# A two-layer attention trunk on one core: gate sums, squares and the last addition change engines, and the list of issue is new

## The chip, the cores and the metric

The kernel runs on one core of one Trainium2 chip. The metric is the device time of one execution in microseconds (us), lower is better. Three executions of the kernel before gave 297.03, 297.08 and 297.94 us, median 297.08. A fourth execution was profiled: it took 296.7 us, of which the profile covers a span of 294.8 us from its first to its last instruction.

## What is computed

The reference is a decoder trunk of two layers over one sequence of 256 tokens, 1024 wide, in fp32:

```
c_act = silu(c)
for layer in range(2):
    shift, scale, gate = split(c_act @ w_ada[layer] + b_ada[layer], 3)
    h = rms_norm(x, norm_g[layer]) * (1 + scale) + shift
    y = even_mixer(h, ...) if layer == 0 else odd_mixer(h, ...)
    x = x + gate * y
return rms_norm(x, final_g)
```

The even mixer projects h with one matrix of 1024 x 2968, runs 8 heads of window attention with sinks and 8 heads of sparse attention (compressed, selected and window branches), multiplies each branch by a SiLU gate path and projects the result with a 1024 x 1024 matrix. The odd mixer does the same with 16 heads of block attention. At this length the selected blocks cover everything that the causal mask leaves, so the kernel computes causal attention there. What matters for the change: gate is a row of 1024 numbers for each layer, made of c_act and a 1024 x 1024 block of w_ada; each rms_norm needs the sum of squares of every row of x; and the output is rms_norm of the x that the second layer leaves.

## The kernel before

The 256 tokens are two tiles of 128 partitions. Weights are 70 MB and are read once. A product in fp32 precision is made of three passes: every operand is split into a rounded part (hi, written by ScalarE as a CAST) and a rest (lo, written by VectorE as a subtraction), and `mm3` (line 576) issues hi x hi, hi x lo and lo x hi. So each 128 x 1024 block of weights costs one ScalarE CAST (`whi<-raw`), one VectorE TENSOR_TENSOR (`wlo<-raw,whi`) and TensorE's three passes over it. Five buffers `raw` take the weights from DMA, four `whi` and four `wlo` hold the split ones; of TensorE's eight accumulators three are called `ps_pj`, two `ps_s`, and one each `ps_pt`, `ps_o` and `ps_m`.

All engine calls go through a recorder (`Plan`, its `record` at line 226), which numbers them and notes what each depends on. `issue` (line 256) then emits them in the order of a long list of numbers, `ORDER` (line 38 on). This list sets how the work of the stages is interleaved on every engine and in which order SP issues the DMAs; each engine then works its own instructions off strictly in that order. Since all instructions leave through one line of the recorder, the profile shows L253 for nearly everything, and the names of the tiles tell what an instruction is.

The stages in order of time, with the names that the prediction uses:

- Start: the norm of x, the shift and scale of layer 0 and the projection of most of the even columns, as the weights arrive.
- The softmax stage of layer 0: six groups of four heads' scores. For each group TensorE makes scores, VectorE takes the row minimum (CUSTOM_DVE, listed as ISA in the order), ScalarE the exponential, VectorE and ScalarE scale (`sm<-sm,rc`), TensorE transposes and multiplies with the values. Gate paths (`ps_pj<-hhi,whi` of 256 columns), and, from `jobs` (line 1164) by `fill`, the ada work are put between.
- The ada work makes rows of c_act @ w_ada in one of two ways, chosen by a letter in `G0_ON`, `SS_ON` and `G1_ON` (lines 26 to 28). Letter "v" (`ada_sums`, line 446): for 512 columns, eight blocks of `raw` are each multiplied by a column of c and summed up in the tile `acc`, the first on ScalarE, the other seven on VectorE (SCALAR_TENSOR_TENSOR `acc<-raw,cz,acc`); for a gate, `ada_gate` (line 504) splits acc, and two matmuls with a matrix of ones (`ones_r`) sum over the partitions. Letter "p" (`ada_rows`, line 429): for 256 columns, eight matmuls on TensorE (`ps_m<-raw,cz`) make partial rows, ScalarE copies them (`asb`), and one matmul with `selbc` adds them up and spreads them.
- The projection out of layer 0 (`out_proj`, line 1188), in two halves of 512 columns. Its second half goes to `ps_s`, one accumulator for each tile of tokens. `add_scaled` (line 378) multiplies by gate, adds to x (the tile `xs`) and sums squares into `parts`.
- The boundary: for each tile of tokens, `inv_root` (line 402) raises the mean square to the power -1/2 on GpSimd, VectorE scales the first 512 columns of x (`t<-xs,parts`) and ScalarE the others, TensorE transposes them (`ta` holds the identity), and the result is scaled, shifted and split into `hhi` and `hlo`, the operands of layer 1.
- Layer 1 in the same manner, and its projection out (from line 1257), whose last piece is tile 1's columns 768 to 1023. Behind it stands the end of the kernel: add x, square with a sum, square root, reciprocal, multiply by `final_g` (`fg`, in `bigA`) and by the reciprocal, and two DMAs, of columns 0 to 383 from ScalarE's queue and of the rest from SP's.

Of the kernel before, what the change touches and what calls it, by code (L numbers as in the profile page):

```python
# [13 lines left out]
P = 128  # L14
# [12 lines left out]
G0_ON = "vp"  # L27
# [237 lines left out]
def tile_trunk(  # L265
# [136 lines left out]
    def inv_root(part):  # L402
        G.tensor_tensor(part[:, 3:4], part[:, 2:3], ex0[:, 0:1], ALU.pow)
        return part[:, 3:4]
# [952 lines left out]
```

## Time and profile before

| what | value |
|---|---|
| median of three executions | 297.08 us (297.03 to 297.94) |
| the profiled execution: its time, its span | 296.7 us, 294.8 us |
| TensorE matmul / weight load busy | 284.1 us (96%) / 242.6 us (82%) |
| VectorE / ScalarE / GpSimd busy | 246.0 (83%) / 194.6 (66%) / 9.1 us (3%) |
| chain that ended last: TensorE, DMA, VectorE | 88%, 4%, 3% |
| mean granted clock of TensorE | 0.99 |

An instruction's row in the profile gives its start and its length in us. The engines overlap the end of one instruction with the beginning of the next, so two rows of one engine in a row start closer together than the first is long; what an added instruction costs is the distance of the starts. PE is TensorE's matmul, PEld its weight load, DVE is VectorE, ACT ScalarE, POOL GpSimd; SPq and ACTq are DMAs issued by SP and by ScalarE. An fp32 matmul that isn't split appears as two rows.

### The profile page before, as it was taken

The page shows a single profiled execution, that of the slowest core. Times are in us where ns is not written, and L with a number is a line of the kernel's source. Part 1 is how long each engine was busy: PE and PEld are TensorE (multiplying, and loading weights), DVE is VectorE, ACT ScalarE, POOL GpSimd, SP SyncE. Part 2 cuts the span into 40 slices and gives each one's busy share as a digit, 9 for nine tenths or more (in the row PEclk, how much of TensorE's full clock was granted, in tenths as well). Part 3 has the DMA queues.
Part 4 walks back from the last instruction along what each step waited for, and adds up shares of the span by engine and source line. Part 5 has one row for each costly group of instructions (what it writes and reads, how often), then busy time and mean ns, then how long its engine had stood idle before and what let it go on. Part 6 is the DMA issues. An engine that isn't in the chain of part 4 may idle for free.

```text
span 294.8 us, 6255 instructions
## 1 busy us (share of the span) xinstructions
PE 284.1 (96%) x2326; PEld 242.6 (82%) x2326; DVE 246.0 (83%) x580; ACT 194.6 (66%) x461; POOL 9.1 (3%) x34
## 2 busy tenths in 40 slices
PE   6899999999999999999999999999999999999991
PEld 5677887999698877777757899999789989887891
DVE  0388798899999999989999569798846998899963
ACT  3477356765899999994458753664488358783832
POOL 4200000001000000000020000000000000000000
PEclk9799999999999999999999999999999999999998
DMA  7999999997799679579989628958466761721003
GB/s 238 374 387 380 374 396 365 353 326 244 211 359 336 230 238 329 194 241 295 286 265 311 201 74 273 344 185 267 143 217 213 218 238 49 259 99 73 0 0 142
DMA packets 62397, 71.69 MB, mean 243 GB/s; under 512 B 3416, under 2 KB 53024, under 8 KB 62368
## 3 DMA queue, kind: packets, MB, share of 16 engines
q1 hardware_dynamic: 61792, 70.78, 72.1%
q10 hardware_dynamic: 448, 0.48, 0.5%
q8 instruction: 18, 0.29, 0.4%
q14 instruction: 11, 0.09, 0.1%
q0 software_dynamic: 128, 0.05, 0.1%
HBM read 70.25 MB, written 1.05 MB: 242 GB/s over the span
## 4 chain that ended last, share of the span: by engine, by line
PE 88%; DMA 4%; DVE 3%; SPq 2%; issue 1%; POOL 1%; ACT 0%; DVEq 0%; ACTq 0%
PE ps_pj L253 57%; PE ps_s L253 11%; PE ps_pt L253 8%; PE ps_o L253 7%; PE ps_m L253 5%; DMA raw<-in_w_in_even_dram 2%; DMA qT<-in_w_ada_dram 2%; SPq L253 2%; DVE acc L253 1%; DVE t L253 1%; POOL parts L253 1%; DVE xs L253 0%; DVE wlo L253 0%; ACT whi L253 0%; ACT t L253 0%
## 5 line engine op out<-in xcount | busy, mean ns | idle before, releaser
L253 ACT CAST whi<-raw 128x1024 fp32r<-128x1024 f32 (+4 forms) x84 | 76.1, 917 | 45.8 <-PE ps_pj L253 20.3
L253 DVE TENSOR_TENSOR wlo<-raw,whi 128x1024 fp32r<-128x1024 f32 (+3 forms) x84 | 87.8, 1056 | 13.1 <-ACT whi L253 13.0
L253 PE MATMUL ps_pj<-hhi,whi 128*128 128x256 f32 x272 | 67.0, 284 | 0.0
L253 PE MATMUL ps_pj<-hlo,whi 128*128 128x256 f32 x272 | 66.7, 282 | 0.0
L253 PE MATMUL ps_pj<-hhi,wlo 128*128 128x256 f32 x272 | 66.6, 284 | 0.0
L253 PEld LDWEIGHTS ps_pj<-hhi,whi 128*128 128x128 f32 x272 | 47.9, 188 | 1.4 <-issue 0.7
L253 PEld LDWEIGHTS ps_pj<-hlo,whi 128*128 128x128 f32 x272 | 47.9, 188 | 0.8 <-issue 0.4
L253 PEld LDWEIGHTS ps_pj<-hhi,wlo 128*128 128x128 f32 x272 | 47.7, 188 | 0.3
L253 DVE SCALAR_TENSOR_TENSOR acc<-raw,cz,acc 128x512 f32<-128x512 f32 x42 | 31.3, 746 | 0.5 <-ACT acc L253 0.3
L253 ACT ACTIVATE sm<-sm,mn 128x256 f32<-128x256 f32 (+1 forms) x58 | 25.9, 449 | 4.9 <-DVE mn L253 4.9
L253 PE MATMUL ps_pj<-whi,hlo 128*128 128x512 f32 (+1 forms) x56 | 21.6, 396 | 0.0
L253 PE MATMUL ps_pj<-whi,hhi 128*128 128x512 f32 (+1 forms) x56 | 21.1, 398 | 0.5 <-ACT hhi L253 0.5
L253 PE MATMUL ps_pj<-wlo,hhi 128*128 128x512 f32 (+1 forms) x56 | 21.5, 396 | 0.0
L253 PE MATMUL ps_pj<-wlo,ghi 128*128 128x512 f32 (+1 forms) x56 | 20.4, 370 | 0.0
L253 PE MATMUL ps_pj<-whi,ghi 128*128 128x512 f32 (+1 forms) x56 | 20.0, 366 | 0.0
L253 PE MATMUL ps_pj<-whi,glo 128*128 128x512 f32 (+1 forms) x56 | 19.9, 364 | 0.0
L253 PE MATMUL ps_pt<-ta,sm 128*128 128x128 f32 x87 | 15.5, 277 | 0.0
L253 DVE TENSOR_TENSOR t<-ps_pj,tF 128x512 f32<-128x512 f32 x18 | 11.6, 683 | 4.5 <-PE ps_pj L253 4.5
L253 ACT COPY pT<-ps_pt 128x384 f32<-128x384 f32 x25 | 11.8, 474 | 3.0 <-PE ps_pt L253 2.7
L253 ACT ACTIVATE t<-xs 128x512 f32<-128x512 f32 (+2 forms) x9 | 6.1, 679 | 11.4 <-DVE xs L253 8.1
L253 PEld LDWEIGHTS ps_pt<-ta,sm 128*128 128x128 f32 x87 | 10.2, 140 | 3.2 <-issue 1.0
L253 PEld LDWEIGHTS ps_pj<-whi,hhi 128*128 128x128 f32 x56 | 10.4, 189 | 2.6 <-ACT hhi L253 0.7
(252 smaller groups left out, 590.9 us busy)
## 6 DMA issues: line engine op xcount, KB each, us to landing
raw<-in_w_in_odd_dram SPq DMA_DIRECT2D x32, 512.0 KB, 5.0
raw<-in_w_ada_dram SPq DMA_DIRECT2D x28, 512.0 KB, 5.7
raw<-in_w_in_even_dram SPq DMA_DIRECT2D x10, 512.0 KB, 7.1
t<-in_w_ada_dram SPq DMA_DIRECT2D x16, 256.0 KB, 5.8
raw<-in_w_out_even_dram SPq DMA_DIRECT2D x8, 512.0 KB, 6.0
raw<-in_w_out_odd_dram SPq DMA_DIRECT2D x8, 512.0 KB, 5.5
raw<-in_w_in_even_dram SPq DMA_DIRECT2D x8, 396.0 KB, 6.0
qT<-in_w_ada_dram SPq DMA_DIRECT2D x12, 256.0 KB, 6.0
```

The source lines that it names most:

```text
L253: self.ops.append(dict(key=eng.key, deps=deps, fn=lambda: getattr(real, name)(*args, **kw)))
```

## The change

The letters for layer 0's gate become "vv": the second 512 columns are now summed on VectorE and ScalarE like the first, not on TensorE. The sum of squares over the last half of x before the boundary is made by a ScalarE activation with an accumulator in place of a VectorE instruction with one, and `inv_root` adds the two halves first, with one small VectorE instruction. In the last piece of the kernel TensorE starts the accumulator with x itself, as identity times the split x (two matmuls), so that the square and the multiplication by `final_g` read the accumulator directly. And `ORDER` is another list. The few words that go with the change also name the second tile's scalings on ScalarE; the diff has no line that moves a scaling, and the lists of instructions hold the same scalings on the same engines before and after.

```
-G0_ON = "vp"
+G0_ON = "vv"
...
 ORDER = [int(i) for i in """
-0 4 74 8 10 3 5 11 2 12 9 6 13 1 14 15 7 77 16 17 34 75 59 60 22 35 61 36 18 19 44 62 38 30 81 45 78 20 21 46 63
...
         elif last:
-            V.tensor_tensor_reduce(
-                out=yt,
...
-                accum_out=part[:, 2:3],
-            )
+            A.activation(yt, xs[:, t, cs], AF.Square, scale=D**-0.5, accum_out=part[:, 2:3])
         else:
...
     def inv_root(part):
+        V.tensor_tensor(part[:, 2:3], part[:, 2:3], part[:, 0:1], ALU.add)
         G.tensor_tensor(part[:, 3:4], part[:, 2:3], ex0[:, 0:1], ALU.pow)
...
+    A.copy(hhi[:, 0, :P], ident)
+    A.copy(hhi[:, 1, :], xs[:, 1, 768:])
+    V.tensor_tensor(hlo[:, 1, :], xs[:, 1, 768:], hhi[:, 1, :].bitcast(F32), ALU.subtract)
...
+            held = done and t == 1
+            plan.fence("pe")
+            if held:
+                T.matmul(py[:, :256], hhi[:, 0, :P], hhi[:, 1, :], start=True, stop=False)
+                T.matmul(py[:, :256], hhi[:, 0, :P], hlo[:, 1, :], start=False, stop=False)
...
+            if held:
+                A.activation(t4()[:, :256], py[:, :256], AF.Square, scale=D**-0.5, accum_out=part[:, 1:2])
+                V.tensor_tensor(xs[:, t, cs], py[:, :256], fg[:, cs], ALU.mult)
+            else:
+                add_scaled(t, cs, py[:, : c1 - c0], part, done, n == 1)
+                V.tensor_tensor(xs[:, t, cs], xs[:, t, cs], fg[:, cs], ALU.mult)
```

Counted over the whole lists, TensorE loses 16 matmuls `ps_m<-raw,cz` and 2 `ps_m<-asb,selbc`, and gains 2 with `ones_r` and the 2 that bring in x. VectorE gains 7 `acc<-raw,cz,acc` and one `wlo<-acc,whi` of 512 columns, one multiplication of gate rows of 512 columns takes the place of two of 256, and 2 sums of squares go. ScalarE gains one `acc<-raw,cz`, one `whi<-acc` and 2 squares, and loses 2 copies `asb`; it also gains the 2 CASTs, and VectorE the subtraction, that split the identity and x near the end. SP issues as many DMAs as before. Between VectorE's first row minimum and its scaling of tile 0 at the boundary stand all of the 7 added sums: 35 rows `acc<-raw,cz,acc` there, 28 before.

The new list moves nearly everything by some places. Three places matter below. TensorE at the boundary, before: rows `ps_s_92` are tile 1's projection, `ps_pj_95<-ta,t_87` and `ps_o_97<-ta,t_87` tile 0's transposes, and `hhi` stands for the first rows of layer 1.

```order
L253 MATMUL ps_s_92<-wlo_114,ghi 128x512
L253 MATMUL ps_pj_95<-ta,t_87 128x128 x4
L253 MATMUL ps_s_92<-whi_110,glo 128x512
L253 MATMUL ps_o_97<-ta,t_87 128x128
L253 MATMUL ps_m_67<-ta,asb_107 128x128
L253 MATMUL ps_s_92<-whi_111,ghi 128x512
L253 MATMUL ps_m_67<-ta,asb_107 128x128
L253 MATMUL ps_s_92<-wlo_115,ghi 128x512
L253 MATMUL ps_s_92<-whi_111,glo 128x512
L253 MATMUL ps_s_92<-whi_111,ghi 128x512
L253 MATMUL ps_s_92<-wlo_115,ghi 128x512
L253 MATMUL ps_s_92<-whi_111,glo 128x512
```

The same place on TensorE after:

```order
L253 MATMUL ps_s_92<-wlo_116,ghi 128x512
L253 MATMUL ps_s_92<-whi_112,glo 128x512
L253 MATMUL ps_m_67<-raw_105,cz 32x256 x8
L253 MATMUL ps_pj_95<-ta,t_87 128x128 x4
L253 MATMUL ps_o_97<-ta,t_87 128x128
L253 MATMUL ps_m_67<-ta,asb_107 128x128 x2
L253 MATMUL ps_o_97<-ta,t_87 128x128 x3
L253 MATMUL ps_m_67<-raw_101,cz 32x256 x8
L253 MATMUL ps_pj_93<-whi_109,hhi 128x512
```

Before, 7 matmuls of tile 1's projection stand behind tile 0's first transposes; after, all of them stand ahead of these, and behind them only transposes and one group of ada rows come before layer 1.

VectorE at the same boundary, before: `ps_s_91,gate` is tile 0's last product with gate, the ISA rows are the sum of squares, and the TENSOR_SCALAR is tile 0's scaling, which waits for GpSimd's power.

```order
L253 TENSOR_TENSOR t_89<-ps_s_91,gate 128x512
L253 TENSOR_TENSOR shs<-ps_m_67,rT 128x2
L253 TENSOR_TENSOR xs<-t_89,xs 128x512
L253 TENSOR_TENSOR shs<-ps_m_67,rT 128x2
L253 ISA t_89,parts<-xs,parts 128x512
L253 ISA parts 128x1
L253 TENSOR_TENSOR wlo_116<-raw_104,whi_112 128x1024
L253 TENSOR_SCALAR t_87<-xs,parts 128x512
```

And after:

```order
L253 TENSOR_TENSOR xs<-t_89,xs 128x512
L253 TENSOR_TENSOR wlo_113<-raw_104,whi_109 128x1024
L253 TENSOR_TENSOR parts<-parts 128x1
L253 TENSOR_TENSOR shs<-ps_m_67,rT 128x2
L253 TENSOR_TENSOR t_90<-ps_s_92,gate 128x512
L253 TENSOR_SCALAR t_87<-xs,parts 128x512
```

The split of weights stood beside GpSimd's power and now stands ahead of the small addition that the power waits for; tile 1's product with gate (`t_90<-ps_s_92,gate`), which stood behind the scaling, now stands beside the power.

The end of the program on VectorE, after; `ps_pj_94` is the last piece's accumulator, which now holds x too.

```order
L253 TENSOR_TENSOR xs<-ps_pj_93,xs 128x256
L253 TENSOR_TENSOR xs<-ps_pj_94,bigA 128x256
L253 TENSOR_TENSOR xs<-xs,bigA 128x256
L253 RECIPROCAL parts<-parts 128x1
L253 TENSOR_SCALAR t_87<-xs,parts 128x640
```

Before, the second row was `xs<-ps_pj_94,xs`, the addition, and the reciprocal stood ahead of the multiplication by `final_g`; now both multiplications stand ahead of the reciprocal.

More of the change, by code (lines that the diff above doesn't have):

```diff
@@ L387, in add_scaled @@
         elif last:
-            V.tensor_tensor_reduce(
-                out=yt,
-                in0=xs[:, t, cs],
-                in1=xs[:, t, cs],
-                scale=1.0 / D,
-                scalar=part[:, 0:1],
-                op0=ALU.mult,
-                op1=ALU.add,
-                accum_out=part[:, 2:3],
-            )
+            A.activation(yt, xs[:, t, cs], AF.Square, scale=D**-0.5, accum_out=part[:, 2:3])
         else:
@@ L1270, in tile_trunk @@
             py = bank("pj")
-            plan.fence("pe")
-            for k in range(KT):
-                mm3(py[:, : c1 - c0], ghi[:, k, sl], glo[:, k, sl], ws[n][k][0][:, c0:c1], ws[n][k][1][:, c0:c1], k == 0, k == KT - 1)
             cs = slice(512 * n + c0, 512 * n + c1)
@@ L1276, in tile_trunk @@
             done = n == 1 and c1 == 512
-            add_scaled(t, cs, py[:, : c1 - c0], part, done, n == 1)
-            V.tensor_tensor(xs[:, t, cs], xs[:, t, cs], fg[:, cs], ALU.mult)
+            held = done and t == 1
[3 more added lines that the diff above has]
+                T.matmul(py[:, :256], hhi[:, 0, :P], hlo[:, 1, :], start=False, stop=False)
+            for k in range(KT):
+                mm3(py[:, : c1 - c0], ghi[:, k, sl], glo[:, k, sl], ws[n][k][0][:, c0:c1], ws[n][k][1][:, c0:c1], k == 0 and not held, k == KT - 1)
+            if held:
[4 more added lines that the diff above has]
+                V.tensor_tensor(xs[:, t, cs], xs[:, t, cs], fg[:, cs], ALU.mult)
             if done:
```

251 rows, old and new, of the table ORDER are left out of this document.

## The prediction

> **What bounds the kernel now.** I read the page first: its shares say which engines can be bounds at all.
>
> ```profile
> span 294.8 us, 6255 instructions
> PE 284.1 (96%) x2326; PEld 242.6 (82%) x2326; DVE 246.0 (83%) x580; ACT 194.6 (66%) x461; POOL 9.1 (3%) x34
> ```
>
> A share over the whole span mixes stages, so next come the windows, cut where the stages meet: the first scores at 72.5 us and tile 0's scaling at 150.8 us. The columns are the window, its length, then busy time and count of PE, PEld, DVE, ACT and POOL, the clock, the DMA share and GB/s.
>
> ```profile
> 20.00:72.50 52.50, 52.37 (x396) 46.03 (x394) 47.58 (x89) 31.39 (x69) 0.60 (x5) 1.00 1.02 351
> 72.50:120.00 47.50, 47.50 (x532) 38.11 (x533) 46.16 (x174) 45.28 (x148) 0.59 (x2) 1.00 0.88 289
> 120.00:150.80 30.80, 30.80 (x198) 22.74 (x194) 28.71 (x57) 21.76 (x49) 1.73 (x3) 1.00 0.77 237
> 160.00:210.00 50.00, 50.00 (x411) 46.30 (x410) 40.17 (x80) 27.30 (x49) 0.00 (x0) 1.00 0.65 208
> 210.00:288.60 78.60, 78.60 (x614) 70.18 (x612) 65.63 (x137) 50.13 (x111) 0.74 (x3) 1.00 0.42 141
> ```
>
> From 160 us on TensorE alone is full. In the softmax stage three engines are: VectorE is busy 46.16 + 28.71 = 74.87 of 78.3 us up to the boundary, ScalarE 45.28 of the first 47.5. A row of PE covers a pipelined matmul, so its busy time alone proves nothing; the timeline of TensorE in that stage (start, length, instruction, count) tells more.
>
> ```profile
> 99.73 0.28 PE L253 MATMUL ps_pj<-hhi,wlo 128*128 128x256 f32 x1
> ...
> 100.31 0.28 PE L253 MATMUL ps_pj<-hhi,wlo 128*128 128x256 f32 x1
> 100.52 1.07 PE L253 MATMUL ps_m<-raw,cz 128*32 128x256 f32 x16
> 101.53 0.66 PE L253 MATMUL ps_pt<-ta,t 128*128 128x128 f32 x4
> ...
> 102.96 0.59 PE L253 MATMUL ps_m<-asb,selbc 128*128 128x256 f32 x2
> 103.39 0.49 PE L253 MATMUL ps_pt<-ta,sm 128*128 128x128 f32 x3
> ```
>
> Starts follow without a hole: five steps of 0.58 / 5 = 0.116 us for 256 columns, 1.01 us for one group of ada rows, 0.43 us for one `selbc`. So TensorE is full there too. The kernel is bound by TensorE nearly throughout, with VectorE and ScalarE right behind it from 72 to 151 us; that is where the change puts work on the second and takes it from the first.
>
> **TensorE's sum.** A matmul of 512 columns costs 0.23 us by these two starts:
>
> ```profile
> 147.13 0.40 PE L253 MATMUL ps_s<-wlo,ghi 128*128 128x512 f32 x1
> 147.36 0.40 PE L253 MATMUL ps_s<-whi,glo 128*128 128x512 f32 x1
> ```
>
> Removed: two groups of ada rows, 2 x 1.01, and two `selbc`, 2 x 0.43: 2.88 us. Added: two matmuls with `ones_r`, 0.46, and the two that bring in x, 2 x 0.116 = 0.23. Net -2.2 us. The list moves other work across the stages, and counting its rows gives this split. Ahead of the first scores stand 7 fewer matmuls of 256 columns: -0.8 us, in a window where TensorE was busy 52.37 of 52.5. Between the first scores and tile 0's transposes stand those 7 and 7 matmuls of tile 1's projection out, so there -2.88 + 0.46 + 0.81 + 1.61 = 0.0. After the transposes: -1.61 + 0.23 = -1.4.
>
> **VectorE's sum.** All of its added work lies between the first scores and the boundary. Its timeline in the stage:
>
> ```profile
> 103.70 0.75 DVE L253 SCALAR_TENSOR_TENSOR acc<-raw,cz,acc 128x512 f32<-128x512 f32 x1
> 104.37 1.22 DVE L253 TENSOR_TENSOR wlo<-raw,whi 128x1024 fp32r<-128x1024 f32 x1
> 105.50 0.42 DVE L253 TENSOR_TENSOR gate<-ps_m,gate 128x256 f32<-128x256 f32 x1
> 105.84 0.68 DVE L253 SCALAR_TENSOR_TENSOR oT<-ps_o,oT 128x512 f32<-128x512 f32 x1
> 106.44 0.74 DVE L253 SCALAR_TENSOR_TENSOR acc<-raw,cz,acc 128x512 f32<-128x512 f32 x1
> ```
>
> By the starts a sum step costs 0.67, two inputs of 512 columns 0.60, the gate step of 256 columns 0.34. So: 7 x 0.67 = 4.7; the low part of the new acc 0.6; one gate step of 512 for two of 256, 0.6 - 0.7 = -0.1; tile 1's product with gate, moved ahead of the scaling, +0.6; the sum of squares that goes, -0.67 (148.43 to 149.10, below); the small addition, some 0.1. Together +5.2 us, where the windows leave 78.3 - 74.9 = 3.4 us idle. If all idle is used the stretch grows by 1.8; if none, by 5.2. It can also stay at TensorE's sum, 0.0: a row ends some 0.08 us after the next may start (0.75 shown, 0.67 spaced), so pauses shorter than that between the 231 rows don't show as idle. I take +1.2, between TensorE's 0.0 and the 1.8, since a new list is free to fill pauses of both kinds. ScalarE's first sum step, CAST and squares less two copies are under 2 us by its own rows of like size, the squares at the boundary; I take them as hidden.
>
> **The boundary.** Rows from the timelines of the engines; brackets give the idle time before an instruction and who ended it.
>
> ```profile
> 146.86 0.69 DVE L253 TENSOR_TENSOR t<-ps_s,gate 128x512 f32<-128x512 f32 x1 [0.18 <-PE ps_s L253]
> 148.43 0.75 DVE L253 CUSTOM_DVE_ANT_0 t<-xs,parts 128x512 f32<-128x512 f32 x1
> 149.10 1.22 DVE L253 TENSOR_TENSOR wlo<-raw,whi 128x1024 fp32r<-128x1024 f32 x1
> 149.26 1.48 POOL L253 TENSOR_TENSOR parts<-parts,expo 128x1 f32<-128x1 f32 x1 [2.22 <-DVE parts L253]
> 149.62 0.63 ACT L253 ACTIVATE t<-xs 128x512 f32<-128x512 f32 x1
> 150.77 0.49 DVE L253 TENSOR_SCALAR t<-xs,parts 128x512 f32<-128x512 f32 x1 [0.45 <-POOL parts L253]
> 151.32 0.66 PE L253 MATMUL ps_pj<-ta,t 128*128 128x128 f32 x4 [0.47 <-DVE t L253]
> 153.12 0.41 ACT L253 CAST hhi<-t 128x256 fp32r<-128x256 f32 x1 [1.63 <-DVE fs L253]
> 154.96 0.48 PE L253 MATMUL ps_pj<-whi,hhi 128*128 128x512 f32 x1
> 156.39 0.55 POOL L253 TENSOR_TENSOR parts<-parts,expo 128x1 f32<-128x1 f32 x1 [5.49 <-DVE fs L253]
> ```
>
> From the end of tile 0's projection (146.8) to the transposes are 4.5 us, and TensorE runs dry for 0.47 of them. The power took 1.48 us beside VectorE's `wlo` and 0.55 without such company. After the change: product 0.6, two small steps 0.2 (0.16 at most each, as the reciprocal below), addition 0.7; the square on ScalarE (0.63 and reading its sum) runs beside the `wlo` of 1.13 that now stands ahead; the small addition with its hand-overs 0.3, the power 0.55, beside a product that reads an accumulator; scaling 0.5: 4.0 us, and 4.5 if the power still waits for that product's end. The cover ahead of the transposes, 12 matmuls of tile 1 and an ada group, is 12 x 0.23 + 1.0 = 3.8. So the hole there stays at 0.2 to 0.7: no term. The Trainium skill, SBUF — State Buffer, "SBUF: two separate sides", has the lock behind these two rows: a VectorE instruction with two SBUF inputs and a GpSimd one that reads SBUF exclude each other for a whole instruction. By that rule the product, with one input in PSUM, doesn't hold up the power, and the hole would be the shorter; both rows agree with it.
>
> What the hole loses comes behind it. Before, the first row of layer 1 started 154.96 - 151.32 = 3.6 us after the transposes, and 7 matmuls, 1.61 us, filled that; now they stand ahead. What is left to TensorE there is two rows of four transposes, 0.66 each or somewhat less, and an ada group of 1.01, some 2 us, while the first CAST of `hhi` ended 2.2 us after the transposes began (153.53). Tile 1's transposes and the low parts come right after, with the same chance of a hole. I take 0.5 us idle in all, bounds 0 and 1.6.
>
> **The end.** The last matmul, and what follows it on each engine:
>
> ```profile
> 288.34 0.27 PE L253 MATMUL ps_pj<-whi,glo 128*128 128x256 f32 x1
> ...
> 288.65 0.42 DVE L253 TENSOR_TENSOR xs<-ps_pj,xs 128x256 f32<-128x256 f32 x1
> 289.17 0.42 ACT L253 ACTIVATE t<-xs 128x256 f32<-128x256 f32 x1 [1.29 <-DVE xs L253]
> ...
> 290.04 0.16 DVE L253 RECIPROCAL parts<-parts 128x1 f32<-128x1 f32 x1 [0.96 <-ACT parts L253]
> 290.12 0.41 DVE L253 TENSOR_TENSOR xs<-xs,bigA 128x256 f32<-128x256 f32 x1
> ...
> 290.56 0.55 DVE L253 TENSOR_SCALAR t<-xs,parts 128x640 f32<-128x640 f32 x1
> 290.88 0.35 ACTq L253 DMA_DIRECT2D out_dram<-t  x1
> 291.18 0.34 SPq L253 DMA_DIRECT2D out_dram<-t  x1
> ```
>
> The addition goes: the square can start at 288.65, 0.52 earlier, and ScalarE's DMA with it. On VectorE both multiplications (0.34 each) fit before the reciprocal at 289.52, so the last scaling comes 0.52 + 0.44 = 0.96 earlier and SP's DMA too. The span ends 3.62 us after SP's issue; ScalarE's DMA then is the later by 0.14. Gain 0.82 to 0.96, and 0.5 if the square is slower from an accumulator: -0.85. The two CASTs and the subtraction that split x lie in the last window, where ScalarE was busy 50.1 of 78.6 us and VectorE 65.6; nothing.
>
> **The sum.** -0.8 + 1.2 - 1.4 + 0.5 - 0.85 = -1.35 us. The profiled execution took 296.7, so 295.3 against it; the median 297.08 lies 0.4 above, and I give the median: 295.7. About 0.3%, 0.9 us, is what a measurement of this kernel can tell from no change.
>
> **The rivals.** TensorE's sum holds: the stretch up to the boundary keeps its 78.3 us, and layer 1 starts without a hole: -0.8 - 1.4 - 0.85 = -3.05, 294.0. For it speaks that VectorE was busy 97% of the time from 72.5 to 120 us while TensorE's starts followed without a hole, so a full VectorE needn't hold TensorE up; against it, that 5.2 us don't fit into the 3.4 shown.
>
> VectorE takes over, the one on the other side. If the new sums delay row minima and splits as they are, and its idle time of 3.4 us stays, the stretch grows by the whole 5.2: -0.8 + 5.2 - 1.4 + 0.5 - 0.85 = +2.65, 299.7. It decides for slower once the stretch grows by over 3.4 us, that is if less than about half the idle is used up. For it speak VectorE's 97% and 93% in the two windows, and ScalarE's 95%, which leaves no third engine to shift to. The Trainium skill, Perfetto Trace Analysis, "Identifying the Most-Contended Engine", holds matmul busy time a bad measure and goes by the share of weight loads; by that TensorE, with 38.11 of 47.5 and 22.74 of 30.8, isn't the bound from 72 to 151 us, its relief is worth nothing there, and the time would be this rival's. The starts without a hole at 100 us disagree with it for that place.
>
> It cancels out: half to all of the shown idle is used and no more, the stretch grows by 1.8 to 3.5, or the new order of the DMAs at the start costs what the end gains: 295.7 + 0.6 to 295.7 + 2.3, 296.3 to 298.0. The scalings named beside the change are where they were, so they have no term in any case.
>
> **How the numbers follow.** The forecast's case, growth of 0.5 to 1.6, 0.36; TensorE's sum holds, 0.20; it cancels, 0.24; VectorE takes over, 0.20. Faster: 0.36 + 0.20 = 0.56; within 0.3%: 0.24; slower 0.20. The range reaches down to 293.7, just under TensorE's sum, and up to 299.0, which leaves out the upper half of the slow case.
>
> **What would show it.** Right: first scores some 0.8 us earlier than 72.5; from there to tile 0's transposes 78.8 to 80.6 us with VectorE idle under 2; a power of 0.55 us; from the last matmul to the SP issue 1.6 instead of 2.6 us. Wrong: VectorE idle as before and the transposes 3 us later, or TensorE idle over 1.6 us behind them.

## The result, and the profile after

The changed kernel took 296.06 us (median of nine executions, 295.55 to 296.85), the kernel before beside it 297.94 (nine, 297.03 to 298.45): ratio 0.9947, 95% interval 0.993 to 0.9964. Run once more, beside the first experiments, it gave 0.997 (0.9951 to 0.9988). So it is faster by 0.3 to 0.5%, some 0.9 to 1.6 us. The profiled execution of it took 296.06 us, its span is 294.3. The head of its page:

```profile
span 294.3 us, 6208 instructions
PE 283.4 (96%) x2294; PEld 244.1 (83%) x2294; DVE 248.5 (84%) x585; ACT 196.5 (67%) x467; POOL 11.5 (4%) x34
```

TensorE has 0.7 us less, VectorE 2.5 and ScalarE 1.9 more. The windows, cut at the same events as before (first scores, now 72.2; tile 0's transposes, now 151.4; last matmul, now 287.0):

```profile
20.00:72.20 52.20, 52.10 (x390) 45.54 (x389) 47.48 (x89) 31.27 (x68) 0.13 (x2) 1.00 1.00 344
72.20:120.00 47.80, 47.80 (x515) 38.95 (x514) 47.59 (x169) 45.30 (x147) 1.04 (x6) 1.00 0.83 272
120.00:151.40 31.40, 31.33 (x195) 23.32 (x193) 30.96 (x68) 22.75 (x50) 0.91 (x3) 1.00 0.77 242
160.00:210.00 50.00, 50.00 (x412) 46.48 (x411) 40.03 (x77) 28.00 (x50) 0.00 (x0) 1.00 0.77 243
210.00:287.00 77.00, 77.00 (x608) 69.04 (x607) 65.36 (x135) 49.46 (x112) 4.14 (x3) 1.00 0.44 144
```

In the second and third row VectorE is busy 47.59 + 30.96 of 79.2 us: 0.65 us idle where 3.4 were before. The boundary, from the timelines of the engines:

```profile
148.85 1.22 DVE L253 TENSOR_TENSOR wlo<-raw,whi 128x1024 fp32r<-128x1024 f32 x1
150.01 0.16 DVE L253 TENSOR_TENSOR parts<-parts 128x1 f32<-128x1 f32 x1
150.25 0.56 POOL L253 TENSOR_TENSOR parts<-parts,expo 128x1 f32<-128x1 f32 x1 [2.24 <-DVE shs L253]
150.29 1.07 PE L253 MATMUL ps_m<-raw,cz 128*32 128x256 f32 x16
150.30 0.69 DVE L253 TENSOR_TENSOR t<-ps_s,gate 128x512 f32<-128x512 f32 x1
150.91 0.48 DVE L253 TENSOR_SCALAR t<-xs,parts 128x512 f32<-128x512 f32 x1
151.44 0.66 PE L253 MATMUL ps_pj<-ta,t 128*128 128x128 f32 x4
152.75 1.18 PE L253 MATMUL ps_m<-raw,cz 128*32 128x256 f32 x16
153.86 0.50 PE L253 MATMUL ps_pj<-whi,hhi 128*128 128x512 f32 x1
```

The power takes 0.56 us in place of 1.48; beside it VectorE now reads an accumulator (`t<-ps_s,gate`), where before it subtracted two operands in SBUF (e_low_half_at_power tests this). No bracket stands at the transposes: the 0.47 us that TensorE ran dry there are gone. Layer 1 starts 153.86 - 151.44 = 2.42 us behind them, before it was 3.64. And the end:

```profile
287.04 0.28 PE L253 MATMUL ps_pj<-whi,glo 128*128 128x256 f32 x1
287.42 0.38 ACT L253 ACTIVATE t<-ps_pj 128x256 f32<-128x256 f32 x1 [1.39 <-PE ps_pj L253]
...
287.92 0.42 DVE L253 TENSOR_TENSOR xs<-ps_pj,bigA 128x256 f32<-128x256 f32 x1 [2.63 <-ACT t L253]
288.26 0.41 DVE L253 TENSOR_TENSOR xs<-xs,bigA 128x256 f32<-128x256 f32 x1
288.60 0.16 DVE L253 RECIPROCAL parts<-parts 128x1 f32<-128x1 f32 x1
...
289.40 0.34 SPq L253 DMA_DIRECT2D out_dram<-t  x1
289.43 0.36 ACTq L253 DMA_DIRECT2D out_dram<-t  x1
```

VectorE's multiplication doesn't start with the square but waits for it (2.63 us idle, ended by ScalarE's `t`); two multiplications then stand between square and reciprocal. SP's DMA leaves 2.36 us after the last matmul instead of 2.84, ScalarE's 2.39 instead of 2.54.

Stage by stage, all from one profile of each kernel (the starts of the rows named; the last two columns are the later of the two final DMAs, and the span's end). The experiments' rows are told below.

| kernel | first scores at | to tile 0's transposes | to layer 1 | to the last matmul | to the last DMA's issue | to the end |
|---|---|---|---|---|---|---|
| before | 72.45 | 78.87 | 3.64 | 133.38 | 2.84 | 3.62 |
| after | 72.19 | 79.25 | 2.42 | 133.18 | 2.39 | 4.87 |
| e_after_again | 72.60 | 79.22 | 2.42 | 133.01 | 2.39 | 4.86 |
| e_all_old_list | 72.92 | 87.34 | 3.63 | 135.51 | 2.06 | 3.94 |
| e_rows_back | 72.32 | 83.89 | 2.42 | 133.15 | 2.39 | 3.93 |
| e_squares_back | 71.64 | 79.71 | 2.41 | 133.62 | 2.39 | 3.92 |
| e_tail_alone | 73.34 | 78.92 | 3.63 | 134.29 | 2.06 | 3.87 |
| e_tail_back | 71.90 | 79.24 | 2.42 | 132.87 | 2.84 | 4.62 |
| e_product_early | 72.24 | 79.24 | 2.42 | 133.02 | 2.06 | 4.82 |
| e_low_half_at_power | 72.98 | 80.22 | 2.42 | 133.14 | 2.39 | 4.15 |
| e_four_sums_less | 72.32 | 79.26 | 2.41 | 133.02 | 2.39 | 3.91 |
| e_one_pass_less | 72.12 | 79.03 | 2.42 | 132.93 | 2.39 | 4.80 |
| e_both_less | 71.58 | 79.03 | 2.41 | 132.98 | 2.39 | 3.91 |
| e_sums_placed | 72.05 | 84.57 | 3.63 | 133.45 | 2.84 | 3.66 |

The four columns in the middle repeat to 0.2 us between two profiles of the changed kernel. The first and the last don't follow the edits: the first scores come at 71.58 to 72.98 us in the ten profiles with the new list or a variant of it and at 72.05 to 73.34 in the four with the former one, and the last column falls into two groups, 3.62 to 4.15 and 4.62 to 4.87. From the first scores to the last DMA the changed kernel takes 217.24 and 217.04 us, the kernel before 218.73: 1.5 to 1.7 us less. Against the first pair of profiles the end gave 1.25 us of it back.

### The profile page after: what moved, and what is told of

Same layout as the page of the kernel before. It is cut to its first block, busy times and chain, and to the rows that moved or that the text cites. A ratio compares the mean times of both kernels' runs of the same rounds, so it can differ in the third digit from the quotient of the medians.

```text
span 294.3 us, 6208 instructions
## 1 busy us (share of the span) xinstructions
PE 283.4 (96%) x2294; PEld 244.1 (83%) x2294; DVE 248.5 (84%) x585; ACT 196.5 (67%) x467; POOL 11.5 (4%) x34
## 3 DMA queue, kind: packets, MB, share of 16 engines
q1 hardware_dynamic: 61792, 70.78, 72.7%
## 4 chain that ended last, share of the span: by engine, by line
PE 94%; DMA 2%; ACT 1%; DVE 1%; POOL 1%; issue 0%; ACTq 0%; POOLq 0%
PE ps_pj L253 59%; PE ps_s L253 12%; PE ps_pt L253 8%; PE ps_o L253 8%; PE ps_m L253 6%; DMA rows_pe<-in_cmp_pe_v_dram 2%; POOL rows L253 0%; ACT t L253 0%; DVE t L253 0%; ACT hhi L253 0%; ACT whi L253 0%; DVE xs L253 0%; POOL rows_pe L253 0%; DVE shs L253 0%; ACT asb L253 0%
## 5 line engine op out<-in xcount | busy, mean ns | idle before, releaser
L253 DVE TENSOR_TENSOR wlo<-raw,whi 128x1024 fp32r<-128x1024 f32 (+4 forms) x84 | 87.5, 1056 | 9.9 <-ACT whi L253 9.8
L253 DVE SCALAR_TENSOR_TENSOR acc<-raw,cz,acc 128x512 f32<-128x512 f32 x49 | 36.4, 743 | 0.2
L253 PE MATMUL ps_pj<-whi,hhi 128*128 128x512 f32 (+1 forms) x56 | 20.5, 394 | 0.1
L253 PE MATMUL ps_pj<-whi,glo 128*128 128x512 f32 (+1 forms) x56 | 20.6, 368 | 0.0
L253 PE MATMUL ps_pt<-ta,sm 128*128 128x128 f32 x87 | 16.3, 278 | 0.0
L253 POOL TENSOR_TENSOR parts<-parts 128x1 f32<-128x1 f32 x5 | 4.5, 907 | 202.0 <-ACT t L253 202.0
```

The lines of the kernel that those rows point to most:

```text
L253: self.ops.append(dict(key=eng.key, deps=deps, fn=lambda: getattr(real, name)(*args, **kw)))
```

## The experiments

The first question was what sets the stretch from the first scores to the transposes, where the change takes work from TensorE and gives it to VectorE, and what the new list has to do with it. Theory 1: VectorE sets it, theory 2: TensorE's sum sets it, theory 3: only the two ends count. Every ratio is to the kernel before, run beside the experiment.

**e_after_again.** No edit.

> The changed kernel once more, unaltered, as the yardstick for the other kernels of this call. All theories: 0.993 to 0.9964 of the kernel before, as measured first; span 293.8 to 295.0.

Measured: ratio 0.997 (0.9951 to 0.9988), span 294.5. The ratio lies just above the expected range; the two intervals overlap, so the gain is the same within them, and small.

**e_all_old_list.** The changed kernel, its list made from the former one.

```
-                a = sb([P, 512], "acc", 1)
+                a = sb([P, 512], "acc2" if fn is ada_gate and l == 0 and i else "acc", 1)
...
-ORDER (in words): the new list
+ORDER (in words): the former list, each new instruction at the place of the one that it replaces
```

> All three edits, but in the former list of issue: each new instruction stands where the one that it replaces stood, and the second gate sums have an accumulator of their own so that they can. Theory 1 (VectorE fills the stretch from the first scores to the boundary, and only the new list finds room for the sums): the sums bring VectorE 5.2 us, where 3.4 us were idle, so the stretch of 78.8 us grows by 1.8 to 5.2; with the tail's 0.5 taken off, 1.3 to 4.7 us slower than before, ratio 1.004 to 1.016. Theory 2 (TensorE's sum sets the stretch): some 2 us of matmuls less and the tail's 0.5, ratio 0.990 to 0.994. Theory 3 (the ends alone count, the gate's sums nothing): 0.995 to 0.998.

Measured: 1.0316 (1.0287 to 1.0346), far beyond all three. The stretch has 87.34 us. Theories 2 and 3 fall for this list; theory 1 has the sign, but the size, 8.5 us for at most 5.2 us of work, suggests that the place of the sums was bad as well; e_sums_placed tries another. Another 2.1 us are lost in layer 1, from a cause that stays open.

**e_rows_back.** The changed kernel with the former way of making the second 512 gate columns.

```
-G0_ON = "vv"
+G0_ON = "vp"
...
-ORDER (in words): 1 mul, 7 sum steps and the split
+ORDER (in words): 2 x 8 products, 2 copies, 2 broadcasts at the same places; ahead of them, earlier than they were,
+the load of the gate's bias, the copy that makes selbc, and the first gate's two matmuls and addition
```

> The changed kernel and its list, with the second 512 columns of layer 0's gate back on TensorE (16 products and 2 broadcasts at the place of the sums). VectorE has 5.2 us less to do, TensorE some 2.0 us more. Theory 1: VectorE set the stretch, so it shortens until TensorE's sum does, and that has 4.2 us of gaps in it: 0 to 2.2 us faster than the changed kernel. Theory 2: TensorE's 2.0 us are added: 298 or so, ratio to before near 1.001. Theory 3: as the changed kernel within 0.5 us.

Measured: 1.0097 (1.0069 to 1.0125), 3.7 us slower than the changed kernel beside it. The stretch grew by 4.65 us although VectorE had 5.2 us less to do: theory 1 falls in its plain form, the gate sums are not nothing (theory 3), and theory 2 has the sign with less than half of the size. VectorE's timeline where the rows stand:

```profile
104.55 0.42 DVE L254 TENSOR_TENSOR gate<-ps_m,gate 128x256 f32<-128x256 f32 x1 [1.99 <-PE ps_m L254]
104.89 1.22 DVE L254 TENSOR_TENSOR wlo<-raw,whi 128x1024 fp32r<-128x1024 f32 x1
106.02 0.48 DVE L254 TENSOR_SCALAR sm<-sm,rc 128x128 f32<-128x128 f32 x2
110.70 0.42 DVE L254 CUSTOM_DVE_ANT_0 sm<-ps_s,tb 128x256 f32<-128x256 f32 x1 [4.20 <-PE ps_pt L254]
```

VectorE stands for 1.99 and 4.20 us: first for the rows' own result (`ps_m`), then for TensorE's next scores, which come at 106.87 to 110.0 us with one group of rows, at 107.95, in their midst. The rows' own 2.4 us (2.88 less the two matmuls with `ones_r`, by the prediction's durations) are half of the 4.65. The rest I put down to this displacement, in which my places for the rows have a part; how large a part is not shown.

**e_squares_back.** The changed kernel with VectorE's sums of squares at the boundary.

```
-            A.activation(yt, xs[:, t, cs], AF.Square, scale=D**-0.5, accum_out=part[:, 2:3])
+            V.tensor_tensor_reduce(
+                out=yt,
...
+                accum_out=part[:, 2:3],
+            )
...
     def inv_root(part):
-        V.tensor_tensor(part[:, 2:3], part[:, 2:3], part[:, 0:1], ALU.add)
```

> The changed kernel and its list, with the last sums of squares before the boundary back on VectorE (0.67 us by the starts each) and without the two small additions (about 0.1 each). Theory 1: one of them stands ahead of tile 0's transposes and one behind: the transposes come 0.5 us later, the end 0.5 to 1.2 us later than in the changed kernel. Theory 2: VectorE's share is hidden, 0 to 0.2 us. Theory 3 (the boundary is one of the ends that count): as theory 1.

Measured: 0.9952 (0.9934 to 0.997), no slower than the changed kernel. By the stages it is: transposes 0.46 us later after the scores, layer 1 another 0.4 to 0.6 longer, 0.9 to 1.1 in all, as theory 1 said. The time (295.98 us beside 296.78) doesn't show it: in the profile the first scores came early (71.64) and the end has the short form (3.92, not 4.86), and I know of no way from the squares to either. So the squares on ScalarE are worth about 1 us by the stages of the trace; the times alone don't show it.

Next the end and the boundary by themselves. Theory A is the forecast's term for the end, theory B what the trace of the changed kernel shows of its issue, theory C that the DMAs give it back.

**e_tail_alone.** The kernel before with the end's edit only: the three preparing instructions, the two matmuls and the `held` branch of the change's diff, each at the place of what it replaces in the former list.

> The kernel before and its list, with the tail's edit alone: TensorE adds x to the last 256 columns, square and multiplication read PSUM. Theory A (the forecast's term): the final DMAs go out 0.52 and 0.96 us earlier after the last matmul, 0.6 to 0.85 us in all, ratio 0.997 to 0.998. Theory B (the multiplication waits for the square, as in the changed kernel's trace: 0.48 from the last matmul to SP's DMA, less 0.24 for two more matmuls of 256 columns): ratio 0.999. Theory C (the two final DMAs now go out together and land later, 4.9 instead of 3.62 us from SP's issue to the end): nothing or up to 1.0 us slower, ratio 1.000 to 1.0035.

Measured: 1.0023 (1.0008 to 1.0039): no gain, if anything 0.7 us slower. From the last matmul to the last DMA 0.78 us are won (2.84 to 2.06), but the way to the last matmul is 0.9 longer: by the starts of the same rows in both kernels, 0.44 of it appears between 257 and 266 us, where the preparing instructions were put, 0.24 is the two matmuls, and the other 0.2 was not traced.

**e_tail_back.** The changed kernel with the end as before (the reverse edit).

> The changed kernel and its list, with the tail as before: no addition by TensorE, VectorE adds x. Against the changed kernel, which took 0.9947 and 0.997 of before: theory A 0.6 to 0.85 us slower, theory B 0.25 slower, theory C up to 1.0 us faster.

Measured: 0.9956 (0.994 to 0.9973), as the changed kernel. The stages: 0.14 to 0.3 us won ahead of the last matmul, 0.45 lost behind it. Theory B's 0.25 fits, theory A falls. The long form of the end is there as well (4.62) though the two DMAs go out 0.29 us apart again, so theory C is not what makes it long.

**e_product_early.** One place in the list: number 2954 is VectorE's multiplication of columns 512 to 767.

```
-2926 2974 2975 2976 2977 2978 2953 2979 2980 2981 2982 2983 2954 2984 ...
+2926 2974 2954 2975 2976 2977 2978 2953 2979 2980 2981 2982 2983 2984 ...
```

> The changed kernel, with one VectorE instruction moved in the list: the multiplication of the piece before (columns 512 to 767) by final_g goes ahead of the last piece's, where VectorE was idle for 2.63 us. The reciprocal then follows the square root without the 0.34 us of that multiplication between: reciprocal 0.34 earlier after the last matmul (1.22 instead of 1.56 us), both DMAs too. If the end is set by what is issued last, 0.3 us faster than the changed kernel (too little for the timing, to be read from the trace); if it is set by the DMA engines, less.

Measured: 0.9944 (0.9931 to 0.9957), the best ratio of the versions that compute everything, not to be told from the changed kernel's. The end's rows:

```profile
286.92 0.28 PE L254 MATMUL ps_pj<-whi,glo 128*128 128x256 f32 x1
287.30 0.38 ACT L254 ACTIVATE t<-ps_pj 128x256 f32<-128x256 f32 x1 [1.39 <-PE ps_pj L254]
...
287.80 0.42 DVE L254 TENSOR_TENSOR xs<-ps_pj,bigA 128x256 f32<-128x256 f32 x1 [1.43 <-ACT t L254]
288.14 0.15 DVE L254 RECIPROCAL parts<-parts 128x1 f32<-128x1 f32 x1
...
288.98 0.36 ACTq L254 DMA_DIRECT2D out_dram<-t  x1
```

The reciprocal comes 1.22 us after the last matmul (288.14 - 286.92), as expected, the last DMA 2.06 instead of 2.39. Read from the trace this is 0.33 us for one number moved.

**e_low_half_at_power.** Number 1690 is the low half that stood ahead of the small addition (1628).

```
-... 1557 1624 1690 1691 1628 1617 1460 1618 1619 ...
+... 1557 1624 1691 1628 1617 1460 1618 1690 1619 ...
```

> The changed kernel, with the low half of 1024 columns (two inputs in SBUF, 1.22 us) moved behind the small addition at the boundary, so that it runs beside GpSimd's power as before the change. If VectorE's two SBUF inputs keep GpSimd out, the power takes 1.2 to 1.5 us instead of 0.56; if they don't, 0.56. In both cases VectorE waits some 0.9 us for the square and then scales 1.0 us later, so tile 0's transposes come 1.0 us later; the end by 0 (TensorE has tile 1's matmuls and an ada group to fill it) to 1.0 us.

Measured: 0.9962 (0.9944 to 0.9979), not to be told from the changed kernel by the times; by the stages 0.97 to 1.0 us longer, all of it ahead of the transposes.

```profile
150.79 0.16 DVE L254 TENSOR_TENSOR parts<-parts 128x1 f32<-128x1 f32 x1 [1.08 <-ACT t L254]
150.94 1.22 DVE L254 TENSOR_TENSOR wlo<-raw,whi 128x1024 fp32r<-128x1024 f32 x1
151.03 1.54 POOL L254 TENSOR_TENSOR parts<-parts,expo 128x1 f32<-128x1 f32 x1 [2.24 <-DVE shs L254]
152.67 0.47 DVE L254 TENSOR_SCALAR t<-xs,parts 128x512 f32<-128x512 f32 x1
153.20 0.66 PE L254 MATMUL ps_pj<-ta,t 128*128 128x128 f32 x4 [1.06 <-DVE t L254]
```

The same power takes 1.54 us beside `wlo` and 0.56 beside a product that reads an accumulator: this is now one edit, and no longer a comparison of two lists. The Trainium skill, SBUF — State Buffer, "SBUF: two separate sides", has that exclusion; the trace agrees. And TensorE stands for 1.06 us: of the cover ahead of the transposes the changed kernel has nothing left over, since a scaling 1.0 us later makes the transposes 1.0 us later.

Then the stretch once more, by leaving work out: theory 1 VectorE, theory 2 TensorE, theory 3 the two in turn.

**e_four_sums_less.**

```
-        for k in range(4):
+        for k in (0, 3) if cols[0] == 20 and l == 0 else range(4):
```

> The changed kernel, with four of the seven VectorE steps of the new gate sums left out (so part of layer 0's gate is not computed), all else and the list the same. VectorE has 4 x 0.67 = 2.7 us less to do in the stretch from the first scores to tile 0's transposes (79.25 us). Theory 1 (VectorE sets the stretch: it was idle for 0.65 us in it): the stretch shortens by 2 to 2.7 us, to 76.5 to 77.2. Theory 2 (TensorE's sum sets it): 79.2, no change. Theory 3 (the two wait for each other in turn, so neither alone sets it): between, about 78.

**e_one_pass_less.**

```
     def mm3(o, shi, slo, mhi, mlo, first, last, less=False):
         T.matmul(o, shi, mhi, start=first, stop=False)
-        T.matmul(o, shi, mlo, start=False, stop=False)
+        if not less:
+            T.matmul(o, shi, mlo, start=False, stop=False)
...
+        less = w is W0 and c0 == 2456 + 256
...
```

> The changed kernel, with one of the three matmul passes of one gate projection (columns 2712 to 2967 of layer 0's second input part) left out: 16 matmuls of 256 columns, 0.12 us each by their starts, 1.9 us of TensorE, and none of VectorE's work. That projection's low half is so not multiplied. Theory 1: the stretch stays 79.2 us. Theory 2: 1.9 us shorter, 77.3. Theory 3: about 78.5.

**e_both_less.** Both edits.

> Both of the kernels before together: four sum steps and the one pass left out. Theory 1: as with the sums alone, 76.5 to 77.2. Theory 2: as with the pass alone, 77.3. Theory 3: more than the two apart add up to, 76.5 or less, 0.9% off the changed kernel's time.

Measured: stretches of 79.26, 79.03 and 79.03 us, where the changed kernel has 79.25. VectorE relieved by 2.7 us of work (four of the seven steps, so a part of the gate is not computed): nothing. TensorE relieved by 1.9 (16 matmuls of one projection): 0.2. Both: 0.2. All three theories fall. (The ratios, 0.9926 with 0.9911 to 0.994, 0.9944 with 0.9926 to 0.9961, 0.9911 with 0.9894 to 0.9928, follow the short form of the end in the first and the third.) The sums over the windows from 98.2 to 120 us, 21.8 us in which the work left out stands: first the changed kernel, then the three in their order.

```profile
sum 21.80, PE 21.80 PEld 17.22 DVE 21.80 ACT 21.68 POOL 0.00; mean PE 5.45 PEld 4.30 DVE 5.45 ACT 5.42 POOL 0.00
```

```profile
sum 21.80, PE 21.80 PEld 17.26 DVE 20.32 ACT 21.68 POOL 0.00; mean PE 5.45 PEld 4.31 DVE 5.08 ACT 5.42 POOL 0.00
```

```profile
sum 21.80, PE 20.64 PEld 15.51 DVE 21.79 ACT 21.80 POOL 0.00; mean PE 5.16 PEld 3.88 DVE 5.45 ACT 5.45 POOL 0.00
```

```profile
sum 21.80, PE 20.71 PEld 15.54 DVE 20.95 ACT 21.80 POOL 0.00; mean PE 5.18 PEld 3.89 DVE 5.24 ACT 5.45 POOL 0.00
```

In the changed kernel all three engines are full. Take 2.7 us from VectorE, and VectorE is idle; take 1.9 from TensorE, and TensorE is; take both, and both are, while ScalarE stays at 21.80 of 21.80. What TensorE then waits for, in the kernel with one pass less, is ScalarE's copies out of `ps_pt` and the buffers behind them:

```profile
PEld ps_pt L253 <- ACT pT L253: 1.5, 3, 0.8
PEld ps_pt L253 <- ACT bigA L253: 0.7, 2, 0.4
```

So ScalarE looks like what holds this part once the other two are eased. The DMAs, the other candidate, don't show: from 72 to 151 us the waits of these four profiles list none that a DMA ended. No kernel took work from ScalarE, so its part is argued, not shown; by the first sum line the other two would be in the way at once.

**e_sums_placed.** The kernel before with the gate's edit only, the sums spread one at a time, much as the new list spreads them.

```
-G0_ON = "vp"
+G0_ON = "vv"
...
-                a = sb([P, 512], "acc", 1)
+                a = sb([P, 512], "acc2" if fn is ada_gate and l == 0 and i else "acc", 1)
...
+ORDER (in words): the former list; the second pair of loads 45 to 139 places earlier, the sum steps one at a time
+behind small VectorE instructions, the two broadcast matmuls where the second copy and broadcast stood
```

> The kernel before and its list, with the gate's second sums on VectorE alone, and these placed better than in e_all_old_list: the second half's loads 0.5 to 1 of a projection earlier, the eight steps among VectorE's small instructions of the third and fourth scores, one at a time, the two broadcast matmuls where the second ada group stood. If the 8.5 us that the sums cost in e_all_old_list came from their place, the stretch (78.9 us in the kernel before) comes to 77 to 80 and the time to 0.993 to 1.005 of before; if the former list has no room for them at any near place, 83 or more and 1.015 or more.

Measured: 1.0197 (1.0172 to 1.0222), a stretch of 84.57 us: the second case. Its windows at the place:

```profile
98.00:100.00 2.00, 1.79 (x14) 1.34 (x13) 1.57 (x6) 2.00 (x5) 0.00 (x0) 1.00 0.92 292
100.00:102.00 2.00, 0.64 (x6) 0.44 (x4) 1.97 (x11) 1.65 (x5) 0.00 (x0) 1.00 0.04 13
102.00:104.00 2.00, 0.30 (x1) 0.14 (x1) 2.00 (x7) 0.62 (x3) 0.00 (x0) 1.00 0.00 0
104.00:106.00 2.00, 1.74 (x9) 1.74 (x10) 2.00 (x12) 1.29 (x4) 0.00 (x0) 0.61 0.00 0
106.00:108.00 2.00, 2.00 (x13) 1.53 (x12) 2.00 (x7) 1.12 (x6) 0.00 (x0) 0.54 0.00 0
```

From 100 to 104 us VectorE is full (1.97, 2.00) and TensorE dry, waiting for VectorE's `t`:

```profile
102.48 0.30 PE L253 MATMUL ps_pt<-ta,t 128*128 128x128 f32 x1 [1.84 <-DVE t L253]
104.26 0.79 PE L253 MATMUL ps_pt<-ta,t 128*128 128x128 f32 x3 [1.48 <-DVE t L253]
```

Here VectorE has taken over, the rival on the other side. It costs more than VectorE's 5.2 us less the 3.4 idle; one part of the rest is that the dry time is followed by 4 us at a granted clock of 0.61 and 0.54.

## Why the prediction was right, point by point

The time (296.06; 295.7 was forecast) is right, and in part by luck: the stretch and the hole came out 1.3 us better than forecast, the end 0.4 worse, and in the profile another 1.25 us that no term had were lost behind the last DMA.

- **Ahead of the first scores, -0.8.** The two profiles give -0.26. Over all profiles the ten with the new list have 71.58 to 72.98, mean 72.2, the four with the former one 72.05 to 73.34, mean 72.7: -0.5, with a scatter as large as the term. A part of the scatter goes with TensorE's granted clock: windows of 0.5 us over the first 20 us show it at 0.50 for 6.8 us in some profiles (both of the changed kernel, e_tail_alone, e_low_half_at_power), for 3.4 us in others (before, e_squares_back, e_one_pass_less, e_both_less, e_sums_placed) and not at all in the other five. Within each of these groups the new list's first scores are earlier by 0.75, 0.47 and 0.72 us on the mean. So the first pair, a long spell against a short one, understates the term, and 0.5 to 0.75 is the better reading of the -0.8; the groups are small, and since the profiles without a spell aren't the earliest, the clock alone doesn't explain the scatter.
- **The stretch, +1.2 with TensorE's sum at 0.0 and 1.8 if all shown idle is used.** Measured +0.38, near the lower bound, with 0.65 us of VectorE's 3.4 left idle. TensorE's 2.4 us of relief were spent, as counted, on the 7 matmuls moved up from behind the transposes and the 7 moved back from the start. The reasoning took VectorE's idle time as what sets the growth, with TensorE's sum as the lower bound; that step failed: with 2.7 us taken off VectorE the stretch keeps its 79.26 us, and with 1.9 off TensorE it loses 0.2. ScalarE, which the forecast took as hidden, is full there as well: 21.85 of 22.0 us from 98 to 120 us before, 21.88 after. That it came out at +0.38 is the list's doing: with the same sums in the former list, at the places that I chose, the stretch grew by 5.7 to 8.5 us.
- **After the transposes, -1.4, and a hole of 0.5.** Measured -1.22 up to layer 1 and -0.2 to -0.37 from there, -1.42 to -1.59 with TensorE's 0.23 for x in it, and no hole: the 0.5 was at its lower bound.
- **The boundary.** The power at 0.55 and no term ahead of the transposes: 0.56, and the 0.47 us of before gone. The squares on ScalarE are worth about 1 us here by the stages of e_squares_back, 0.46 of it ahead of the transposes; the forecast had one of the two, as 0.67 in VectorE's sum.
- **The end, -0.85.** This failed. Right was that the addition goes and the square starts earlier, 0.38 us behind the last matmul where it was 0.83. Wrong was that both multiplications "fit before the reciprocal at 289.52", 1.18 behind the last matmul: it came 1.56 behind it. The first of them reads the same accumulator as the square and waits for it, so SP's DMA left 0.48 earlier, not 0.96, ScalarE's 0.15, not 0.52; less 0.24 for TensorE's two matmuls the edit is worth 0.2 us, and by itself in the former list nothing. The sign that was named, 1.6 us from the last matmul's end to SP's issue, came out as 2.08 (289.40 - 287.32). The Trainium skill, PSUM — Partial Sum Buffer, "PSUM bank collisions raise a hardware error", says that two engines must be kept from reading one bank at once; the row with 2.63 <-ACT agrees, and the forecast should have had it.
- **Behind the last DMA, no term.** Measured +1.25 in the first pair of profiles. See below; it is no part of the edits.

From the first scores to the last DMA the forecast had +1.2 - 1.4 + 0.5 - 0.85 = -0.55, and measured were -1.5 to -1.7: the stretch 0.8 better, the hole 0.5, the end 0.4 worse. Ahead of it the first pair shows less than forecast, and behind it over 1 us was lost, so that the whole came close to -1.35 by terms that cancel. By its numbers the rival in which TensorE's sum holds was the nearer one (+0.38 in the stretch against its 0.0, and no hole); its 294.0 was missed because the two ends gave little. Its mechanism isn't borne out either: taking 1.9 us from TensorE shortened the stretch by 0.2.

## What to carry to other kernels

Where three engines are full at once, what moving work between two of them is worth can hang on the order more than on the sum: with the gate's sums in it the stretch grew by 0.4 us in the list made for them and by 5.7 in the former list with the sums put in by hand, and the rows that they replaced, put by hand into the new list, cost 4.6. Price such a change by its list, look at the third engine too, and leave some work out of one engine to see which of them holds the rest. Effects under 1 us are better read between two events inside the program than from its time, which here carries a start that scatters by 1 us and an end with two forms. When a step's input moves into an accumulator, count who else reads that accumulator at that moment.

## What the runs showed of the hardware that was not expected

The two groups of the last column go with one packet. The DMA view of the 3.5 us from SP's issue on (289.4 to 292.9), of the changed kernel:

```profile
DMA  0000000004979999989999996110100000000000
q14 instruction: 1, 0.01, 0.6%
out_dram<-t ACTq DMA_DIRECT2D x1, 192.0 KB, 3.6
```

and of e_squares_back, whose end has the same instructions:

```profile
DMA  0000000004979999999999995100000000000000
out_dram<-t ACTq DMA_DIRECT2D x1, 192.0 KB, 2.6
```

In the first a packet of the queue for instructions (8 KB, at 291.24 us) falls among the output's; the transfers of one or so of the 16 engines (the last digits are 1) come later, and the landing takes 3.6 us instead of 2.6. In the five profiles with such a packet there, the span ends 4.62 to 4.87 us after the last DMA's issue; in the nine without, 3.62 to 4.15. The changed kernel had it both times, e_squares_back, e_four_sums_less and e_both_less not. That the packet is the cause fits all fourteen, but no kernel was made to move it, so it is not shown. If it is, the changed kernel without it would be some 0.9 us faster, an estimate from 4.86 against 3.92.

TensorE's granted clock falls to about half after TensorE runs dry: in e_sums_placed two windows with 0.64 and 0.30 of 2 us busy were followed by two at 0.61 and 0.54, which costs an estimated 2 x 0.39 + 2 x 0.46 = 1.7 us of TensorE's full speed. The Trainium skill, TensorE: Matmul & The Clock Gate, "HAM oscillation — how this bites in real kernels", names idle of over some 3.4 us as what brings the half clock; here less was enough. In e_sums_placed the longest pauses were 1.84 and 1.48 us with one matmul between them, and in e_all_old_list the clock stood at 0.50 from 106.3 to 109.7 us after 3.4 us in which TensorE was busy for 1.80, with no pause over 1.08. In the changed kernel's windows from 20 to 287 us the clock stays at 1.00, as in the kernel before.
